# A transformer block on one core: seven products of quarters for eight in half of the second feed-forward

## The chip, the cores and the metric

The kernel runs on one core of a Trainium2 chip. The metric is the device time of one execution in microseconds. The kernel before takes 2150.8 us, the median of 3 runs (2146.12 to 2152.6).

## The reference

A block over 256 tokens of width 2048, in fp32: a gated feed-forward, a mixer (a state-space layer beside pooling), cross-attention to a memory of 256 rows, a second gated feed-forward, and a final norm. The change is in the second feed-forward alone, which is

```
def swiglu(x, w_gate, w_up, w_down):
    return (jax.nn.silu(x @ w_gate) * (x @ w_up)) @ w_down
h = h + 0.5 * swiglu(rmsnorm(h, g_ffn2[l]), w2_gate[l], w2_up[l], w2_down[l])
return rmsnorm(h, g_final)
```

with w_gate and w_up of 2048 x 5632 and w_down of 5632 x 2048.

## The kernel before, in words

The products are done in two rounded parts each. A weight tile of 512 input channels x 512 columns (1 MB) is loaded into one of three buffers `raw` by SyncE's queue. `wtile` splits it in two halves: for each, ScalarE rounds it to `whi` (L134) and VectorE subtracts what was rounded off, `wlo` (L135), both 128 x 1024 elements. `whi` and `wlo` have three buffers each, so three halves can be on the way. The activations are split in the same way, `xh` and `xl`, and stay in memory. `tok_block` then multiplies a channel block of 128 with both token tiles (lt = 0 and 1): xh x whi, xh x wlo, xl x whi, six matmuls of 512 columns in PSUM (L148 to L150). A half is two channel blocks, 12 matmuls; a unit of 512 channels is 24.

The feed-forward goes over 11 chunks f of 512 inner columns. A chunk's gate is four units over the 2048 channels (`tok_unit`), its up four more. ScalarE takes a tanh of the gate's sum (L302), VectorE makes the gated activation `s` from it (L304, L309), TensorE transposes `s` (L284, eight matmuls of 128 columns), and the two engines split the result into `x` tiles (L180, L181). After each two or three chunks (PASSES) come the down products: for each of four column groups one unit per chunk, whose sum VectorE adds to `h` (L256). The transposes are held back until the next unit has begun (`late`, `held`).

The order of the instructions on each engine is set when the kernel is built: a scheduler runs a model of the program and places each engine's instructions in the order in which they come up there. On the chip each engine then takes its own list strictly in that order.

Of the kernel before, what the change touches and what calls it, by code (L numbers as in the profile page):

```python
# [14 lines left out]
P = 128  # L15
# [7 lines left out]
FC = NQ  # L23
PASSES = ((0, 3), (3, 6), (6, 9), (9, 11))
# [29 lines left out]
def block_kernel(ctx: ExitStack, tc: tile.TileContext, xT, memT, wgu1, wd1, w_in, w_glu, w_pool, w_out,  # L54
# [10 lines left out]
    psA = ctx.enter_context(tc.tile_pool(name="psA", bufs=6, space=bass.MemoryType.PSUM))  # L65
    psB = ctx.enter_context(tc.tile_pool(name="psB", bufs=2, space=bass.MemoryType.PSUM))
# [60 lines left out]
    def wtile(load):  # L127

        raw = wraw.tile([P, 4, 512], F32, name="raw")
        load(raw)  # L130
        blocks = []
# [34 lines left out]
    def total(acc, out=None):  # L166
        b = ev.tile([P, L], F32, name="evb")
        S.activation(out=b, in_=acc[:, L:], func=AF.Copy)
        t = ev.tile([P, L], F32, name="evt", bufs=3) if out is None else out
        V.tensor_tensor(out=t, in0=acc[:, :L], in1=b, op=ALU.add)  # L170
        return t
# [85 lines left out]

    def ffn(fe, wgu, wd, xs, aside=None, begin=None, before=None, after=None):
# [21 lines left out]
        def transposed(ss, acts, t):  # L280
            pt = psB.tile([P, 2, L], F32, name="psb")
            for j in range(2):
                for lt in range(2):
                    T.transpose(pt[:, j, lt * P:(lt + 1) * P], ss[lt][:, (2 * t + j) * P:(2 * t + j + 1) * P], ident)  # L284
            for j in range(2):
                acts.append(split(ap_, pt[:, j]))

        for a, b in PASSES:
            acts = []
            for f in range(a, b):  # L290
# [4 lines left out]
                if f == 0:  # L295
                    norm_of_h()
                    V.tensor_scalar(out=hcol, in0=rcol, scalar1=0.5, scalar2=None, op0=ALU.mult)
                    V.tensor_scalar(out=qcol, in0=rcol, scalar1=0.25, scalar2=None, op0=ALU.mult)
                ss = []
                for lt in range(2):  # L300
                    th = fe.tile([P, 512], F32, name="th", bufs=2)
                    S.activation(out=th, in_=ag[lt], func=AF.Tanh, scale=hcol[:, lt:lt + 1])  # L302
                    s = fe.tile([P, 512], F32, name="s", bufs=4)
                    V.scalar_tensor_tensor(out=s, in0=th, scalar=1.0, in1=ag[lt], op0=ALU.add, op1=ALU.mult)  # L304
                    ss.append(s)
                if au is None:
                    au = tok_unit([cols4(wgu[4 * f:4 * f + 4, 1], i) for i in range(4)], xs, held())
                for lt in range(2):
                    V.scalar_tensor_tensor(out=ss[lt], in0=au[lt], scalar=rcol[:, lt:lt + 1], in1=ss[lt], op0=ALU.mult,  # L309
                                           op1=ALU.mult)  # L310
                late += [lambda ss=ss, t=t: transposed(ss, acts, t) for t in range(2)]
# [299 lines left out]
    kp = ExitStack()  # L611
    kT = kp.enter_context(tc.tile_pool(name="kp", bufs=1)).tile([P, KT, L], F32, name="kT")
    with ExitStack() as c2:
# [35 lines left out]
        def pool_in(n):  # L649
# [12 lines left out]
            q = ev.tile([P, L], F32, name="evs")  # L662
# [6 lines left out]
        def pool_out(g):  # L669
            wpb = load_w(w_pool[g], 512)  # L670
            for m in (2 * g, 2 * g + 1):
                acc = ntile(wpb[m % 2 * 2:m % 2 * 2 + 2], [pooled[2 * g], pooled[2 * g + 1]])
                b = ev.tile([P, L], F32, name="evb")
                S.activation(out=b, in_=acc[:, L:], func=AF.Copy, scale=vcol(P_SCALE + m))
                z = ev.tile([P, L], F32, name="evt", bufs=3)
# [135 lines left out]
        def gelu(j, slots):  # L811
# [6 lines left out]
            th = ev.tile([P, L], F32, name="evth")  # L818
# [41 lines left out]
        for n in range(8):  # L860
# [4 lines left out]
            th = ev.tile([P, L], F32, name="evth")  # L865
# [124 lines left out]
    with tc.tile_pool(name="fe2", bufs=2) as fe:  # L990
        o = fe.tile([P, KT, L], F32, name="o", bufs=1)

        def columns(n):
# [9 lines left out]
        ffn(fe, wgu2, wd2, xf, before=lambda i: layer_in(xf, ND - 1, G_FFN2, [xp] * KT) if i == 3 else None,  # L1003
            after=lambda n, i: columns(n - 1) if n > 0 and i == 1 else None)
# [87 lines left out]
```

## Time and profile before

| | |
|---|---|
| median of 3 runs | 2150.8 us |
| the profiled execution's own time | 2150.47 us |
| its span | 2148.7 us |
| TensorE busy | 2110.9 us (98%) |
| VectorE busy | 1305.9 us (61%) |
| ScalarE busy | 1012.1 us (47%) |
| DMA, mean | 199 GB/s |

The span runs from the first to the last instruction of the profiled execution. Busy time is the sum of the instructions' durations, with overlaps counted once. The second feed-forward lies between about 1406 us and 2132 us of the span. In the rows below PE is TensorE, PEld its weight loads, DVE VectorE, ACT ScalarE, SPq SyncE's queue of transfers; `acc` and `psb` are PSUM tiles.

### The profile page before, as it was taken

What the parts mean: (1) busy time and instruction counts of PE and PEld (TensorE: products, weight loads), DVE (VectorE), ACT (ScalarE), POOL (GpSimd) and SP (SyncE); (2) the same over time, 40 slices, a digit from 0 to 9 for tenths busy, and PEclk for the clock granted to TensorE, in tenths of its full rate; (3) what the DMA queues carried; (4) which work ended last, traced back from release to release, by engine and by line L of the source; (5) the groups of instructions that cost most, each with busy time, mean ns of one, the idle gap of its engine ahead of it and who ended that gap; (6) DMA issues with size and microseconds to landing.
All of it is one profiled execution on the core that took longest, in us unless ns stands there. A gap on an engine that the chain in (4) does not pass through costs nothing.

```text
span 2148.7 us, 26678 instructions
## 1 busy us (share of the span) xinstructions
PE 2110.9 (98%) x10356; PEld 1751.3 (82%) x10356; DVE 1305.9 (61%) x1793; ACT 1012.1 (47%) x1436; POOL 141.4 (7%) x255
## 2 busy tenths in 40 slices
PE   8999999999999999979999999999999999999997
PEld 7888888888888888867888888888888888888886
DVE  6567776766556667736867755555555555555554
ACT  7443444344444546524655644444434444444444
POOL 0000011111100011930000000000000000000000
PEclk9999999999999999989999999999999999999998
DMA  7666776777676666767554545566566656665662
GB/s 246 209 194 190 203 220 223 222 218 212 229 220 187 229 197 218 260 205 236 196 171 163 201 172 176 178 194 182 192 195 191 188 189 196 192 188 189 195 194 100
DMA packets 202320, 427.58 MB, mean 199 GB/s; under 512 B 17873, under 2 KB 31377, under 8 KB 193105
## 3 DMA queue, kind: packets, MB, share of 16 engines
q1 hardware_dynamic: 181280, 392.35, 58.9%
q0 software_dynamic: 6416, 18.85, 3.0%
q10 hardware_dynamic: 14496, 14.68, 2.2%
q8 instruction: 81, 1.33, 0.2%
q14 instruction: 47, 0.38, 0.0%
HBM read 408.05 MB, written 16.78 MB: 198 GB/s over the span
## 4 chain that ended last, share of the span: by engine, by line
PE 93%; POOL 3%; DMA 1%; DVE 1%; issue 1%; ACT 0%; SPq 0%; DVEq 0%; ACTq 0%
PE acc L150 25%; PE acc L148 25%; PE acc L149 25%; PE acc L116 7%; PE acc L117 4%; PE acc L968 1%; PE acc L969 1%; PE acc L967 1%; PE psb L284 1%; POOL big L728 1%; POOL rec L725 1%; POOL rec L726 1%; POOL rec L727 1%; PE psb L245 0%; DMA tab<-WTd 0%
## 5 line engine op out<-in xcount | busy, mean ns | idle before, releaser
L135 DVE TENSOR_TENSOR wlo<-raw,whi 128x1024 fp32r<-128x1024 f32 x576 | 705.9, 1226 | 600.0 <-ACT whi L134 598.0
L134 ACT ACTIVATE whi<-raw 128x1024 fp32r<-128x1024 f32 x576 | 610.9, 1061 | 785.0 <-PE acc L150 730.7
L149 PE MATMUL acc<-wlo,x 128*128 128x512 f32 x2368 | 925.0, 391 | 0.0
L150 PE MATMUL acc<-whi,x 128*128 128x512 f32 x2368 | 923.3, 391 | 0.0
L148 PE MATMUL acc<-whi,x 128*128 128x512 f32 x2368 | 843.8, 391 | 0.0
L150 PEld LDWEIGHTS acc<-whi,x 128*128 128x128 f32 x2368 | 444.8, 188 | 92.3 <-issue 1.2
L149 PEld LDWEIGHTS acc<-wlo,x 128*128 128x128 f32 x2368 | 445.0, 188 | 91.7 <-issue 0.4
L148 PEld LDWEIGHTS acc<-whi,x 128*128 128x128 f32 x2368 | 444.4, 188 | 91.5 <-issue 0.6
L116 PE MATMUL acc<-x,whi 128*128 128x512 f32 x848 | 301.4, 401 | 3.2 <-ACT whi L96 3.2
L97 DVE TENSOR_TENSOR wlo<-raw,whi 128x1024 fp32r<-128x1024 f32 (+1 forms) x144 | 172.0, 1199 | 125.9 <-ACT whi L96 110.0
L117 PE MATMUL acc<-x,wlo 128*128 128x256 f32 x848 | 235.8, 284 | 2.7 <-DVE wlo L97 2.6
L96 ACT ACTIVATE whi<-raw 128x1024 fp32r<-128x1024 f32 (+1 forms) x144 | 146.8, 1023 | 155.4 <-PE acc L116 78.1
L116 PEld LDWEIGHTS acc<-x,whi 128*128 128x128 f32 x848 | 159.0, 189 | 42.3 <-ACT whi L96 5.2
L117 PEld LDWEIGHTS acc<-x,wlo 128*128 128x128 f32 x848 | 159.5, 190 | 8.2 <-DVE wlo L97 5.3
L180 ACT ACTIVATE x<-psb 128x256 fp32r<-128x256 f32 x104 | 36.8, 376 | 46.3 <-PE psb L284 34.1
L181 DVE TENSOR_TENSOR x<-psb,x 128x256 fp32r<-128x256 f32 x104 | 41.5, 418 | 22.9 <-ACT x L180 22.8
L968 PE MATMUL acc<-wlo,x 128*128 128x512 f32 x128 | 50.1, 391 | 0.4 <-DVE wlo L97 0.4
L256 DVE SCALAR_TENSOR_TENSOR h<-acc,qcol,h 128x512 f32<-128x512 f32 x64 | 45.1, 743 | 6.7 <-PE acc L150 6.7
L969 PE MATMUL acc<-whi,x 128*128 128x512 f32 x128 | 48.8, 391 | 0.0
L967 PE MATMUL acc<-whi,x 128*128 128x512 f32 x128 | 47.9, 390 | 0.0
L302 ACT ACTIVATE th<-acc,hcol 128x512 f32<-128x512 f32 x44 | 30.0, 689 | 22.0 <-PE acc L150 22.0
L304 DVE SCALAR_TENSOR_TENSOR s<-th,acc 128x512 f32<-128x512 f32 x44 | 29.7, 685 | 8.4 <-ACT th L302 8.2
(218 smaller groups left out, 1079.4 us busy)
## 6 DMA issues: line engine op xcount, KB each, us to landing
raw<-in_wgu SPq DMA_DIRECT2D x175, 1024.0 KB, 5.9
raw<-in_wd SPq DMA_DIRECT2D x88, 1024.0 KB, 5.3
raw<-in_w_in SPq DMA_DIRECT2D x16, 1024.0 KB, 4.9
raw<-in_w_k SPq DMA_DIRECT2D x16, 1024.0 KB, 5.1
raw<-in_w_out SPq DMA_DIRECT2D x32, 512.0 KB, 4.9
raw<-in_w_q SPq DMA_DIRECT2D x16, 1024.0 KB, 4.8
raw<-in_w_v SPq DMA_DIRECT2D x16, 1024.0 KB, 4.9
raw<-in_w_o SPq DMA_DIRECT2D x16, 1024.0 KB, 5.1
```

The costliest lines, as they stand in the source:

```text
L96: S.activation(out=hi[:, :n], in_=r, func=AF.Copy)
L97: V.tensor_tensor(out=lo[:, :n], in0=r, in1=hi[:, :n].bitcast(F32), op=ALU.subtract)
L116: T.matmul(acc, w[0], x, start=first, stop=False)
L117: T.matmul(acc[:, :L], w[1], x[:, :L], start=False, stop=last)
L134: S.activation(out=hi, in_=raw[:, :, c:c + 256], func=AF.Copy)
L135: V.tensor_tensor(out=lo, in0=raw[:, :, c:c + 256], in1=hi.bitcast(F32), op=ALU.subtract)
L148: T.matmul(acc, xh, w[0], start=first, stop=False)
L149: T.matmul(acc, xh, w[1], start=False, stop=False)
L150: T.matmul(acc, xl, w[0], start=False, stop=last)
L967: T.matmul(accs[mt], mh, wh, start=k == 0, stop=False)
L968: T.matmul(accs[mt], mh, wl, start=False, stop=False)
L969: T.matmul(accs[mt], ml, wh, start=False, stop=k == KT - 1)
```

## The change

For the chunks f = 2 to 10 the first half of the channels (1024 of 2048) is computed with seven products for eight. The 256 tokens are two tiles, the 1024 channels two quarters of 512, and gate and up are the two column groups; that is a product of 2 x 2 by 2 x 2 blocks. Four of the seven products take differences of weight quarters, which VectorE makes in halves (`less`, L1050), and four take sums or differences of token tiles, which `token_sums` makes once (SH and SL). Each product (`product`) splits its weights into `whi` and `wlo` with `parts` as before, and is four channel blocks of three matmuls (L1057 to L1059). The products' results are added on VectorE, in SBUF (L1117, L1122 to L1124, L1139, L1143). The other half of the channels is done as before, in units (`eight`).

I name the pieces of a chunk in the order of the code: P1 (r11), D1, P2 (r12 - r11), D2, P3 (r22 - r12 + r11), D3, P4, D4, then E1 (gate), P5 (r21), E2 (up), P6 (r22), P7, E3 (gate), E4 (up). D1 to D4 are four down units of the two chunks before, which `seven` takes from the generator `down` one at a time (`step`); a and b are the two halves of each. The passes are now of two chunks, chunks 0 and 1 are computed without products, and the last pass has one chunk. PSUM is divided anew: four tiles `acc`, two `dacc` for the down sums, two `psb`.

```
+PASSES2 = ((0, 2), (2, 4), (4, 6), (6, 8), (8, 10), (10, 11))
...
+    banks.close()
+    psA = ctx.enter_context(tc.tile_pool(name="psC", bufs=4, space=bass.MemoryType.PSUM))
+    psB = ctx.enter_context(tc.tile_pool(name="psD", bufs=2, space=bass.MemoryType.PSUM))
...
+    def less(out, a, b):
+        for c in (0, 256):
+            V.tensor_tensor(out=out[:, :, c:c + 256], in0=a[:, :, c:c + 256], in1=b[:, :, c:c + 256], op=ALU.subtract)
+
+    def product(acc, w, x, first, last):
+
+        acc = acc.rearrange("p (f c) -> p f c", f=4)
+        for j, (wh, wl) in enumerate(parts(w)):
+            xh, xl = x(j)
+            T.matmul(acc, xh, wh, start=first and j == 0, stop=False)
+            T.matmul(acc, xh, wl, start=False, stop=False)
+            T.matmul(acc, xl, wh, start=False, stop=last and j == 3)
...
+            x = wraw.tile([P, 8, L], F32, name="raw")
+            for k in range(8):
+                V.tensor_tensor(out=x[:, k], in0=xf[k][:, :L].bitcast(F32), in1=xf[k][:, L:].bitcast(F32), op=ALU.add)
...
+            s = wraw.tile([P, 4, 4, P], F32, name="raw")
...
+            s1, s5, u2, u3 = (sw.tile([P, 512], F32, name=n) for n in ("s1", "s5", "u2", "u3"))
+            t = sw.tile([P, 4, 512], F32, name="t")
+            r11 = load(wraw, "raw", cols4(g, 0))
+            p = tmp()
+            product(p, r11, quarter(0, 0), True, True)
+            S.activation(out=s1, in_=p, func=AF.Copy)
+            step()
+            r12 = load(sw, "r12", cols4(u, 0))
+            less(t, r12, r11)
+            p = tmp()
+            product(p, t, tsum(0), True, True)
+            S.activation(out=s5, in_=p, func=AF.Copy)
+            step()
+            r22 = load(sw, "r22", cols4(u, 1))
+            less(t, r22, t)
+            p = tmp()
+            product(p, t, tsum(1), True, True)
+            V.tensor_tensor(out=u2, in0=p, in1=s1, op=ALU.add)
+            step()
+            less(r12, r22, r12)
+            p = tmp()
+            product(p, r12, tsum(2), True, True)
+            V.tensor_tensor(out=u3, in0=p, in1=u2, op=ALU.add)
+            V.tensor_tensor(out=u2, in0=u2, in1=s5, op=ALU.add)
+            V.tensor_tensor(out=s5, in0=u3, in1=s5, op=ALU.add)
+            step()
+            gate, up = ([psA.tile([P, 512], F32, name="acc") for _ in range(2)] for _ in range(2))
...
+            eight(gate, g, 2)
+            r21 = load(sw, "r21", cols4(g, 1))
+            product(gate[0], r21, quarter(4, 0), False, False)
+            eight(up, u, 2)
+            product(up[0], r22, tsum(3), False, False)
+            less(t, r21, t)
+            product(gate[1], t, quarter(4, 1), False, False)
+            eight(gate, g, 3)
+            gs_ = [sw.tile([P, 512], F32, name=f"gate{lt}") for lt in range(2)]
+            for lt, x in enumerate((s1, u3)):
+                V.tensor_tensor(out=gs_[lt], in0=gate[lt], in1=x, op=ALU.add)
+            ss = gated(fe, gs_)
+            eight(up, u, 3)
+            for lt, x in enumerate((u2, s5)):
+                V.tensor_tensor(out=gs_[lt], in0=up[lt], in1=x, op=ALU.add)
+            upped(ss, gs_)
+            finish_chunk(ss, acts)
...
-        ffn(fe, wgu2, wd2, xf, before=lambda i: layer_in(xf, ND - 1, G_FFN2, [xp] * KT) if i == 3 else None,
-            after=lambda n, i: columns(n - 1) if n > 0 and i == 1 else None)
+        for n, _ in enumerate(down(*PASSES2[-1], acts, done=squares)):
+            if n > 0:
+                columns(n - 1)
```

On VectorE, in the kernel before, this is the end of a chunk's up units and the beginning of the next chunk (s is the gated activation, x its transposed tiles):

```order
L135 TENSOR_TENSOR wlo_13844<-raw_13837,whi_13843 128x1024
L135 TENSOR_TENSOR wlo_13878<-raw_13875,whi_13877 128x1024
L135 TENSOR_TENSOR wlo_13882<-raw_13875,whi_13881 128x1024
L309 SCALAR_TENSOR_TENSOR s_13727<-acc_13733,rcol_92,s_13727 128x512
L309 SCALAR_TENSOR_TENSOR s_13731<-acc_13734,rcol_92,s_13731 128x512
L135 TENSOR_TENSOR wlo_13934<-raw_13931,whi_13933 128x1024
L135 TENSOR_TENSOR wlo_13938<-raw_13931,whi_13937 128x1024
L181 TENSOR_TENSOR x_13890<-psb_13885,x_13890 128x256
```

On VectorE, now, at the end of chunk 2: E3 (13279, 13283), E4 (13325, 13329), the half differences of chunk 3's t and r12 between them, and P1 of chunk 3 (13369, 13373):

```order
L140 TENSOR_TENSOR wlo_13279<-raw_13276,whi_13278 128x1024
L1050 TENSOR_TENSOR t_13364<-r12_13447,raw_13365 128x4x256 x2
L140 TENSOR_TENSOR wlo_13283<-raw_13276,whi_13282 128x1024
L1050 TENSOR_TENSOR r12_13447<-r22_13509,r12_13447 128x4x256
L140 TENSOR_TENSOR wlo_13325<-raw_13322,whi_13324 128x1024
L1050 TENSOR_TENSOR r12_13447<-r22_13509,r12_13447 128x4x256
L140 TENSOR_TENSOR wlo_13329<-raw_13322,whi_13328 128x1024
L1139 TENSOR_TENSOR gate0_13310<-acc_13140,s1_12867 128x512
L1139 TENSOR_TENSOR gate1_13311<-acc_13141,u3_12870 128x512
L140 TENSOR_TENSOR wlo_13369<-raw_13365,whi_13368 128x1024
L140 TENSOR_TENSOR wlo_13373<-raw_13365,whi_13372 128x1024
L275 SCALAR_TENSOR_TENSOR s_13316<-th_13314,gate0_13310 128x512
```

Where four splits stood side by side, four half differences now stand between them, and the additions of the products' sums follow. The list goes on with s, D1a (13416), two additions (L1143) and D1b (13420); then VectorE has, up to D2a (13476):

```order
L281 SCALAR_TENSOR_TENSOR s_13316<-gate0_13310,rcol_92,s_13316 128x512
L140 TENSOR_TENSOR wlo_13453<-t_13364,whi_13452 128x1024
L281 SCALAR_TENSOR_TENSOR s_13320<-gate1_13311,rcol_92,s_13320 128x512
L140 TENSOR_TENSOR wlo_13457<-t_13364,whi_13456 128x1024
L1050 TENSOR_TENSOR t_13364<-r22_13509,t_13364 128x4x256 x2
L140 TENSOR_TENSOR wlo_13476<-raw_13473,whi_13475 128x1024
L186 TENSOR_TENSOR x_13394<-psb_13389,x_13394 128x256
```

Both halves of P2 (13453, 13457) and the whole next difference stand ahead of D2a. On TensorE, at the same place, D2a (13475, into dacc) stands ahead of P2 (13452, into psb); these are its last two matmuls and P2's first three:

```order
L154 MATMUL dacc_13412<-wlo_13476,x_12904 128x512
L155 MATMUL dacc_13412<-whi_13475,x_12904 128x512
L1057 MATMUL psb_13451<-whi_13452,SH_12214 128x512
L1058 MATMUL psb_13451<-wlo_13453,SH_12214 128x512
L1059 MATMUL psb_13451<-whi_13452,SL_12215 128x512
```

So the two engines have the two pieces in opposite order. A little later on TensorE, at the end of P3 (13518) and the beginning of D3a (13539):

```order
L1059 MATMUL psb_13513<-whi_13518,SL_12215 128x512
L153 MATMUL dacc_13535<-whi_13539,x_12576 128x512
L153 MATMUL dacc_13536<-whi_13539,x_12576 128x512
L1057 MATMUL psb_13573<-whi_13574,SH_12214 128x512
L154 MATMUL dacc_13535<-wlo_13540,x_12576 128x512
L155 MATMUL dacc_13535<-whi_13539,x_12576 128x512
```

The first matmul of P4 (13574) stands in the middle of D3a, ahead of the first that reads D3a's wlo.

## Rows read from the trace of the kernel before

**Rows 1.** The page: busy time of each engine with its share of the span, and the share of the chain that ended last by engine.

```profile
PE 2110.9 (98%) x10356; PEld 1751.3 (82%) x10356; DVE 1305.9 (61%) x1793; ACT 1012.1 (47%) x1436; POOL 141.4 (7%) x255
...
PE 93%; POOL 3%; DMA 1%; DVE 1%; issue 1%; ACT 0%; SPq 0%; DVEq 0%; ACTq 0%
```

**Rows 2.** Two windows of 66 us in the second feed-forward: the stretch, its length, then each engine's busy time (instructions), the granted clock, the share of the DMA engines and GB/s.

```profile
1451.00:1517.00 66.00, 66.00 (x298) 54.66 (x297) 35.88 (x38) 30.36 (x36) 0.00 (x0) 1.00 0.65 191
1737.00:1803.00 66.00, 66.00 (x297) 54.66 (x296) 35.90 (x37) 26.66 (x28) 0.00 (x0) 1.00 0.60 187
```

**Rows 3.** The chain in order of time, second feed-forward: start, length, what.

```profile
1450.66 0.66 PE psb L284 x6
1457.02 0.45 PE acc L148 x2
1459.74 0.45 PE acc L148 x2
...
1495.11 0.65 PE psb L284 x6
```

**Rows 4.** The waits between 1450 and 2090 us: who waited for whom, in total, times, the longest.

```profile
ACT whi L134 <- PE acc L150: 326.2, 212, 1.7
DVE wlo L135 <- ACT whi L134: 284.3, 230, 1.5
```

**Rows 5.** The timeline around 1747 us: start, length, engine, line, operation, and in brackets the idle time before it and what ended it.

```profile
1746.90 0.39 PE L150 MATMUL acc<-whi,x 128*128 128x512 f32 x1
...
1747.13 0.62 PE L148 MATMUL acc<-whi,x 128*128 128x512 f32 x2
...
1747.39 1.06 ACT L134 ACTIVATE whi<-raw 128x1024 fp32r<-128x1024 f32 x1 [1.67 <-PE acc L150]
...
1748.48 1.23 DVE L135 TENSOR_TENSOR wlo<-raw,whi 128x1024 fp32r<-128x1024 f32 x1 [1.50 <-ACT whi L134]
...
1749.62 1.40 DVE L256 SCALAR_TENSOR_TENSOR h<-acc,qcol,h 128x512 f32<-128x512 f32 x2
```

**Rows 6.** Groups by line and shape from 1480 us to the end: count, total busy us, mean ns of one, idle time before.

```profile
L135 DVE TENSOR_TENSOR wlo<-raw,whi 128x1024 fp32r<-128x1024 f32 x234 | 286.6, 1225 | 284.9 <-ACT whi L134 284.5
L134 ACT ACTIVATE whi<-raw 128x1024 fp32r<-128x1024 f32 x233 | 247.0, 1061 | 336.6 <-PE acc L150 324.0 <-issue 12.4
...
L256 DVE SCALAR_TENSOR_TENSOR h<-acc,qcol,h 128x512 f32<-128x512 f32 x32 | 22.5, 744 | 6.7 <-PE acc L150 6.7
L181 DVE TENSOR_TENSOR x<-psb,x 128x256 fp32r<-128x256 f32 x40 | 15.9, 418 | 12.0 <-ACT x L180 12.0
...
L304 DVE SCALAR_TENSOR_TENSOR s<-th,acc 128x512 f32<-128x512 f32 x18 | 12.3, 687 | 4.0 <-ACT th L302 4.0
...
L1009 DVE TENSOR_TENSOR o<-o,Ra 128x1024 f32<-128x1024 f32 x4 | 4.6, 1218 | 1.8 <-ACT Ra L214 1.8
```

**Rows 7.** Timeline of VectorE, two pairs that start back to back (the length is that of the pair).

```profile
1423.98 1.28 DVE L304 SCALAR_TENSOR_TENSOR s<-th,acc 128x512 f32<-128x512 f32 x2 [0.84 <-ACT th L302]
...
1453.81 0.75 DVE L181 TENSOR_TENSOR x<-psb,x 128x256 fp32r<-128x256 f32 x2
```

**Rows 8.** TensorE waiting elsewhere in the kernel: three rows of the timeline around 1010 us (a matmul of 512 columns, a split, and the matmul that reads it), the window around them, the kernel's longest wait, and the window around that.

```profile
1009.22 0.39 PE L116 MATMUL acc<-x,whi 128*128 128x512 f32 x1
...
1010.02 1.22 DVE L97 TENSOR_TENSOR wlo<-raw,whi 128x1024 fp32r<-128x1024 f32 x1
...
1011.29 0.39 PE L117 MATMUL acc<-x,wlo 128*128 128x256 f32 x1 [1.68 <-DVE wlo L97]
...
1008.00:1012.00 4.00, 2.32 (x11) 1.63 (x11) 2.38 (x4) 1.76 (x4) 0.00 (x0) 1.00 0.19 49
...
933.58 0.70 PE L798 MATMUL psb<-tab,big 128*32 128x128 f32 x8 [11.62 <-DMA big<-big]
...
920.00:940.00 20.00, 8.38 (x73) 6.74 (x72) 2.79 (x3) 1.56 (x3) 10.77 (x29) 0.66 0.43 128
```

**Rows 9.** DMA issues between 1744 and 1800 us: count, KB each, median us from issue to landing.

```profile
raw<-in_wd SPq DMA_DIRECT2D x7, 1024.0 KB, 5.3
raw<-in_wgu SPq DMA_DIRECT2D x4, 1024.0 KB, 5.9
```

More of the change, by code (lines that the diff above doesn't have):

```diff
@@ L130, in wtile, with parts @@
         load(raw)
+        return parts(raw)
+    def parts(raw):
         blocks = []
@@ L278, in held @@
             return run
[L280 to L286, printed above, removed]
         for a, b in PASSES:
@@ L295, in ffn @@
                 if f == 0:
[L296 to L305, printed above, removed]
+                    ffn_norm()
+                ss = gated(fe, ag)
                 if au is None:
                     au = tok_unit([cols4(wgu[4 * f:4 * f + 4, 1], i) for i in range(4)], xs, held())
[L308 to L311, printed above, removed]
+                upped(ss, au)
+                late += [lambda ss=ss, t=t: act_tiles(ss, acts, t) for t in range(2)]
             for n in range(ND):
@@ L611, in block_kernel @@
     kp = ExitStack()
+    ev2 = kp.enter_context(tc.tile_pool(name="ev2", bufs=2))
     kT = kp.enter_context(tc.tile_pool(name="kp", bufs=1)).tile([P, KT, L], F32, name="kT")
@@ L987, in block_kernel, with flush @@
     kp.close()
-    with tc.tile_pool(name="fe2", bufs=2) as fe:
-        o = fe.tile([P, KT, L], F32, name="o", bufs=1)
+    banks.close()
+    psA = ctx.enter_context(tc.tile_pool(name="psC", bufs=4, space=bass.MemoryType.PSUM))
+    psB = ctx.enter_context(tc.tile_pool(name="psD", bufs=2, space=bass.MemoryType.PSUM))
+    fe = ctx.enter_context(tc.tile_pool(name="fe2", bufs=2))
+    gate_up = lambda f, m: wgu2[4 * f:4 * f + 4, m]
+    late = []
+    def flush(n=2):
+        for _ in range(min(n, len(late))):
+            late.pop(0)()
@@ new lines, in finish_chunk, with plain, first @@
+    def finish_chunk(ss, acts):
+        late.extend([lambda t=t: act_tiles(ss, acts, t) for t in range(2)])
+    def plain(f, acts, before=None):
+        def first(i):
+            flush()
+            if before is not None:
+                before(i)
+        ag = tok_unit([cols4(gate_up(f, 0), i) for i in range(4)], xf, first)
+        if f == 0:
+            ffn_norm()
+        ss = gated(fe, ag)
+        upped(ss, tok_unit([cols4(gate_up(f, 1), i) for i in range(4)], xf))
+        finish_chunk(ss, acts)
@@ new lines, in down @@
+    def down(a, b, acts, accs_of=tok_accs, done=None):
+        for n in range(ND):
+            accs = accs_of()
+            for i, f in enumerate(range(a, b)):
+                blocks = wtile(cols4(wd2[f, 4 * n:4 * n + 4], 0))
+                flush()
+                for j, w in enumerate(blocks):
+                    tok_block(accs, w, acts[4 * i + j], i + j == 0, f == b - 1 and j == 3)
+                if f == b - 1:
+                    add_to_h(accs, n, qcol)
+                    if done is not None:
+                        done(n)
+                yield
@@ L993, in columns @@
+    with tc.tile_pool(name="last", bufs=1) as last:
+        o = last.tile([P, KT, L], F32, name="o")
         def columns(n):
```

84 lines of the change are left out of this document (75 added, 9 removed).

## The prediction

> **What bounds the kernel now.** I read the page's busy times and its chain first [rows 1]: TensorE is busy for 98% of the span and carries 93% of the chain, VectorE is at 61%, ScalarE at 47%. Then the windows over two pieces of the second feed-forward [rows 2]: TensorE is busy for every one of the 66 us, at a granted clock of 1.00, VectorE for 36 of them. So there it runs on matmuls alone. The chain in order of time [rows 3] gives their price: the same pair of matmuls comes back every 2.72 us (1457.02, 1459.74), and 12 matmuls of 512 columns lie between, so a matmul costs 0.227 us. A chunk's gate and up take 44.45 us (1450.66 to 1495.11), eight transposes in it 0.88 (six of them 0.66); its down blocks are another 96 x 0.227 = 21.8. Sum 66.2 us per chunk.
>
> The waits [rows 4] say what the other engines do meanwhile: ScalarE waits 326 us for TensorE to hand back a weight buffer, VectorE 284 us for ScalarE. That is the slack the change spends. One turn of that loop is in [rows 5]: the last matmul of a half starts at 1746.90, the next half's first at 1747.13; ScalarE starts the next `whi` at 1747.39, which is 0.26 after; it takes 1.06; VectorE starts `wlo` 0.03 later (1748.48) and needs 1.23. From a buffer handed back to a usable `wlo` are 2.6 us.
>
> **What it removes.** Per chunk f = 2 to 10 seven products of 12 matmuls stand for eight: 12 x 0.227 = 2.72 us less. Nine chunks: 24.5 us off TensorE's path.
>
> **What it adds on VectorE.** I name a chunk's pieces: P1 to P7 the products (2.72 us of TensorE each), E1 to E4 the plain units of the other channels (5.44 each), D1 to D4 the woven down blocks (5.44 each), a and b their halves. Before, a chunk had 24 halves to split, now 30, and 8 half differences at L1050, 8 additions of a product's sum, and no other engine takes any of it. The split lasts 1.225 us, the same shape without rounding 1.218 [rows 6]; but back to back they start closer: 1748.48 to 1749.62 is 1.14 [rows 5]. The trace has no L1050; its bounds are 0.59 from below (a shape half as long, the step of the pair at 1423.98 [rows 7]) and 1.23; same shape, engine and memory as `wlo`, so I take 1.14. The 128x512 operations step by 0.59 to 0.66 (pairs of 1.28 and 1.40 less one duration [rows 5 to 7]): 0.63. The transposed tiles step by 0.33 (0.75 less 0.42 [rows 6, 7]). A chunk: 38 x 1.14 + 16 x 0.63 + 4 x 0.33 = 54.7 us, against TensorE's 276 x 0.227 + 0.9 = 63.5. On the average VectorE fits. The question is where.
>
> **Where it doesn't fit (A).** Three weight buffers let VectorE be at most three halves ahead. Take T = 0 when TensorE has done P6. E3a's buffer comes free then, so its `wlo` starts at 0.26 + 1.06 + 0.03 = 1.35. From there the order gives VectorE, without a wait that would be later: E3, E4, P1, D1, P2 and D2a (11 splits), six half differences, and eight 128x512 operations. That is 17 x 1.14 + 8 x 0.63 = 24.4 us; with the last one's full duration and 0.05 to reach TensorE (VectorE ends at 1011.24, TensorE starts at 1011.29 [rows 8]) D2a's `wlo` is there at 25.9. TensorE meanwhile has P7, E3, E4, P1, D1 = 21.8, eight transposes 0.9, two matmuls of D2a 0.45: it stands at 23.1, because D2a is in its order before P2, whose weights have long been ready. Stall 2.8 us. In eight chunks, 3 to 10; before chunk 2 the plain units leave VectorE time, and I count 0.
>
> **The second place (B).** T = 0 when D2a resumes. TensorE: ten matmuls 2.27, P2, D2b and P3 8.16, two of D3a 0.45, one of P4: at 11.1 it wants D3a's `wlo`. VectorE: P3a's buffer, P2a's, is free at 3.63, so its `wlo` starts at 4.98; with P3b, two half differences, two additions to `h` (1.40) that makes D3a's start 4.98 + 4 x 1.14 + 1.3 = 10.9, its end 12.2. Stall 1.1. Even with VectorE quick, P4a's `whi`, which TensorE wants ahead of that, uses P3b's buffer: free at 10.43, ready 1.35 later, wanted at 10.88: 0.9. I take 1.2, in nine chunks. In the chunks where D2b takes P2a's buffer some 0.4 more: 0.2 a chunk on the mean.
>
> **Small things.** The token sums take two of three raw buffers, so one weight load is issued only when the last split of the load before ends, and lands 5.3 to 5.9 us later [rows 9]; with `whi` and `wlo` 8 us, while TensorE has two halves and two matmuls, 5.9, in hand: 2 us, once. The first transposes of the feed-forward follow right on the output projection, so they wait for `h`: 0.3 + 0.74: 1. The last pass has one chunk instead of two, so ScalarE's squares and copies crowd: 1. The loads of r12, r21 and r22 each wait for the last split that reads the old one; r22's is the latest, three us ahead of its use, and I cost it at nothing; if it lands late, VectorE stands still with all its splits behind it. The additions at L1139 wait for E3's last matmul, which has ended some two us before VectorE gets to them: nothing. POOL does nothing here. In the tail nothing is removed.
>
> **Sum.** Against the profiled execution's own time, 2150.5 us (span 2148.7; median of the runs shown 2150.8, no difference): 2150.5 - 24.5 + 8 x 2.8 + 9 x 1.2 + 9 x 0.2 + 2 + 1 + 1 = 2165. A chunk goes from 66.2 to 67.6: it saves 2.7 and waits 4.2. I forecast **2165 us, slower**.
>
> **Rivals.**
> *It simply saves.* VectorE has 54.7 of 63.5 us, and before it waited half its time; if its lead at E3 is larger than three buffers allow on my reading, or the half differences step near their lower bound (8 x 0.55 = 4.4 us less a chunk, more than both stalls), the time is 2150.5 - 24.5 + 4 = 2130. Against it: the buffers' handing back is what VectorE waits for in [rows 4].
> *It cancels.* The operations of A step by 5 to 10% less than I take (1.2 to 2.4 of 24.4 us), B stays, since the buffer alone makes 0.9 of it: 2165 - 8 x 1.2 = 2155 down to 2165 - 8 x 2.4 = 2146, some 2150. For it: the bounds of L1050 lie wide. Against: it is `wlo`'s shape.
> *Slower still: VectorE's operations don't overlap.* Place: the same two; with 1.23 a step instead of 1.14 the 17 + 6 operations of A and B take 2.1 us more, each of it a stall: 2165 + 8 x 2.1 = 2182. It decides from 1.17 a step on (then 2171). For it: several of these operations wait for the one just before them (the difference reads what was just written). Against: all 1.14 in the trace are of pairs that wait for ScalarE too.
> [...]
> [...]
> That the seven products are not fewer matmuls is excluded: the order has 108 fewer of 512 columns.
>
> **How the numbers follow.** Forecast 0.50 (its own range 2157 to 2176), saves 0.20, cancels 0.14, no overlap 0.11, clock 0.05. A measurement of this kernel can tell about 0.3%, 6.5 us, from no change: 2144 to 2157. Faster 0.21 (saves, and the low end of cancels), same 0.15, slower 0.64. The range cuts half of the saving case and the worst of the slow ones: 2136 to 2184.
>
> **What would show it.** In the profile after: TensorE waiting for `wlo` at the matmuls of `dacc`, some 2.8 us once in each chunk with the transposes just ahead, and some 1.2 us at `dacc` or at the product of r12; 67 to 68 us from one chunk's transposes to the next; VectorE without idle time over some 24 us before each long wait; L1050 at 1.2 us. Wrong if TensorE's waits sum to under 15 us, if they are for DMAs, or if the chunk is 64 us.

## The result, and the profile after

The changed kernel takes 2176.1 us in the median of 4 runs (2173.0 to 2180.7), against 2148.6 for the kernel before (2146.1 to 2152.6). The ratio is 1.0128, 95% interval 1.0102 to 1.0155: slower by about 27 us. The forecast was 2165, slower, with 2136 to 2184 as its range. The direction came out as forecast. The size is 11 us short, at the very end of the likeliest case's own range (2157 to 2176).

The profiled execution has a span of 2172.8 us. Its page, as in [rows 1], first the busy time of each engine, then the shares of the chain that ended last:

```profile
PE 2104.4 (97%) x10248; PEld 1733.9 (80%) x10248; DVE 1504.0 (69%) x2021; ACT 1080.7 (50%) x1510; POOL 141.5 (7%) x255
...
PE 86%; DVE 5%; POOL 3%; issue 2%; ACT 2%; DMA 1%; SPq 0%; DVEq 0%; ACTq 0%
```

TensorE runs 108 matmuls fewer (10356 to 10248), as the change says. VectorE has 198 us more to do and now carries 5% of the chain, where it had 1%. On the average it is still far from full (69%). The two windows of [rows 2], with the same columns, show that the average hides where it is full:

```profile
1451.00:1517.00 66.00, 65.31 (x292) 53.56 (x290) 48.14 (x49) 31.79 (x37) 0.00 (x0) 1.00 0.61 180
1737.00:1803.00 66.00, 62.33 (x273) 49.96 (x272) 54.38 (x57) 33.46 (x38) 0.00 (x0) 1.00 0.61 181
```

In the first window little is lost (before, TensorE was never idle there). In the second, deep in the feed-forward, TensorE is idle for 3.67 us and starts 273 matmuls instead of 297 in the same 66 us.

The waits from 1440 to 2100 us, as in [rows 4] (who waited for whom: us in total, times, the longest):

```profile
ACT whi L139 <- PE dacc L155: 121.2, 67, 3.8
DVE wlo L140 <- ACT whi L139: 117.7, 114, 3.9
...
PE dacc L154 <- DVE wlo L140: 17.6, 13, 2.0
...
PE psb L1057 <- ACT whi L139: 5.9, 9, 0.7
```

Read the second row against its counterpart in [rows 4]. VectorE waited 284 us for ScalarE's `whi`; now it is 118. That slack was spent. The third and fourth rows are new: TensorE waits for `wlo`, and for the `whi` of P4, which it did nowhere in the feed-forward before.

The timeline around the first of these places, stall A of chunk 3 (start, length, engine, line, operation; in brackets the idle time before it and who ended it). L140 is the split's subtraction, L153 to L155 the matmuls of a down block, L287 the transposes, L1050 a half difference:

```profile
1564.59 1.22 DVE L140 TENSOR_TENSOR wlo<-t,whi 128x1024 fp32r<-128x1024 f32 x1
...
1565.25 1.03 PE L287 MATMUL psb<-ident,s 128*128 128x128 f32 x8
1565.45 1.06 ACT L139 ACTIVATE whi<-raw 128x1024 fp32r<-128x1024 f32 x1 [1.66 <-PE dacc L155]
...
1565.73 2.35 DVE L1050 TENSOR_TENSOR t<-r,t 128x1024 f32<-128x1024 f32 x2
...
1566.56 0.73 PE L153 MATMUL dacc<-whi,x 128*128 128x512 f32 x2 [0.28 <-ACT whi L139]
1568.00 1.21 DVE L140 TENSOR_TENSOR wlo<-raw,whi 128x1024 fp32r<-128x1024 f32 x1
...
1569.27 0.77 PE L154 MATMUL dacc<-wlo,x 128*128 128x512 f32 x1 [1.97 <-DVE wlo L140]
...
1570.27 0.63 PE L154 MATMUL dacc<-wlo,x 128*128 128x512 f32 x1
1570.69 0.63 PE L155 MATMUL dacc<-whi,x 128*128 128x512 f32 x1
```

This is the picture that the prediction drew for D2a: eight transposes, two matmuls on D2a's `whi` (1566.56), then nothing until its `wlo`, which VectorE begins only at 1568.00 because the two half differences for P3 stand ahead of it. The bracket of 1.97 understates the loss, since it counts from the pair's end in the trace (1567.29), which is 0.28 behind two steps of 0.2267. Counted from starts, the pair at 1566.56 should be followed 0.45 us later, and is followed 2.71 us later: 2.26 lost. The pair itself is 0.47 late. Together 2.73 us.

VectorE over the 24.8 us before that restart, same columns as the other windows:

```profile
1544.50:1569.27 24.77, 22.52 (x104) 18.20 (x102) 24.53 (x27) 12.82 (x15) 0.00 (x0) 1.00 0.55 187
```

It is busy for 24.53 of 24.77 us, in 27 operations. But for 0.17 us ahead of the first that starts there it hardly waits; it works through its queue. Below, two of these operations, neither of which waits for anything:

```profile
1548.16 1.22 DVE L140 TENSOR_TENSOR wlo<-raw,whi 128x1024 fp32r<-128x1024 f32 x1
1549.30 1.22 DVE L1050 TENSOR_TENSOR r<-r,r 128x1024 f32<-128x1024 f32 x1
```

The duration is 1.22 us and the step from one start to the next 1.13 to 1.15.

VectorE's queue is not the whole of A. D2a takes the weight buffer that D1's second half has just handed back: ScalarE waits for that and writes the `whi` from 1565.45 to 1566.51. With VectorE free at that moment its `wlo` would be ready at about 1567.8 (0.03 to start, 1.22, 0.05 to reach TensorE). TensorE would want it at 1566.5, which is 0.45 behind the undelayed start of the pair (1566.09). So of the 2.73 us some 1.5 are, by this estimate, the two half differences' and some 1.3 the buffer's, which TensorE's order brings out by taking D2a straight behind D1. In chunk 2, where P2 stands between them and VectorE has less to do, there is no stall A.

Stall B, some 12 us behind A in the same chunk (L1057 is the first kind of matmul of a product, here P4's):

```profile
1581.61 0.62 PE L153 MATMUL dacc<-whi,x 128*128 128x512 f32 x2
...
1581.94 2.35 DVE L140 TENSOR_TENSOR wlo<-raw,whi 128x1024 fp32r<-128x1024 f32 x2
1582.92 0.50 PE L1057 MATMUL psb<-whi,SH 128*128 128x512 f32 x1 [0.69 <-ACT whi L139]
1583.26 0.46 PE L154 MATMUL dacc<-wlo,x 128*128 128x512 f32 x1
```

P4's first matmul comes 1.31 us behind the start of D3a's pair, of which 0.45 is the pair's own: 0.86 lost. It waits for `whi` by name, and in chunks 4, 6, 8 and 10 D3a's `wlo` then costs 0.94 more.

**Where the time went.** Taking every start of TensorE from 1395 to 2110 us against a step of 0.2267 us for 512 columns (0.105 for a transpose), the kernel before loses about 1 us and the changed one 46.8 us more (such a sum is good to a microsecond or so):

| term | forecast, us | read after, us |
|---|---|---|
| A | 8 x 2.8 = 22.4 | 8 x 2.73 = 21.8 |
| B | 9 x 1.2 = 10.8 | 9 x 0.86 + 4 x 0.94 = 11.5 |
| D2b, where it takes P2a's buffer | 1.8 | 4 x 0.32 = 1.3 |
| wait behind the token sums, once | 2 | 1.7 |
| first transposes wait for `h` | 1 | 0.45 + 0.48 = 0.9 |
| clock low behind A | 0 | 3 x some 1.6 = 4.7 |
| the four products on sums of tokens, slower step | 0 | 2.6 |
| many steps of 0.1 and less | 0 | 2.2 |
| tail, behind 2110 us | 1 | 2.3 |
| sum | 39.0 | 49.1 |

Less the 24.5 us saved that is 24.6 us, and the two spans differ by 24.1. From one chunk's transposes to the next are 68.0 to 70.3 us, 69.0 in the mean (1566.56 to 2049.41 in seven steps), against 66.2 before and the 67 to 68 that the prediction named as its sign.

### The profile page after: what moved, and what is told of

It reads as the page before. It is cut to its first block, busy times and chain, and to the rows that moved or that the text cites. A ratio compares the mean times of both kernels' runs of the same rounds, so it can differ in the third digit from the quotient of the medians.

```text
span 2172.8 us, 26801 instructions
## 1 busy us (share of the span) xinstructions
PE 2104.4 (97%) x10248; PEld 1733.9 (80%) x10248; DVE 1504.0 (69%) x2021; ACT 1080.7 (50%) x1510; POOL 141.5 (7%) x255
## 3 DMA queue, kind: packets, MB, share of 16 engines
q8 instruction: 80, 1.31, 0.2%
## 4 chain that ended last, share of the span: by engine, by line
PE 86%; DVE 5%; POOL 3%; issue 2%; ACT 2%; DMA 1%; SPq 0%; DVEq 0%; ACTq 0%
PE acc L153 18%; PE acc L155 18%; PE acc L154 18%; PE acc L118 7%; PE acc L119 4%; PE dacc L154 3%; PE dacc L155 3%; DVE wlo L140 2%; PE dacc L153 2%; PE acc L984 1%; PE acc L985 1%; PE acc L983 1%; PE psb L1057 1%; PE acc L1057 1%; PE acc L1059 1%
## 5 line engine op out<-in xcount | busy, mean ns | idle before, releaser
L140 DVE TENSOR_TENSOR wlo<-raw,whi 128x1024 fp32r<-128x1024 f32 x522 | 636.0, 1223 | 376.2 <-ACT whi L139 373.8
L154 PE MATMUL acc<-wlo,x 128*128 128x512 f32 x1760 | 688.4, 391 | 0.0
L155 PE MATMUL acc<-whi,x 128*128 128x512 f32 x1760 | 686.8, 391 | 0.0
L153 PE MATMUL acc<-whi,x 128*128 128x512 f32 x1760 | 628.2, 392 | 1.8 <-ACT whi L139 1.6
L153 PEld LDWEIGHTS acc<-whi,x 128*128 128x128 f32 x1760 | 330.3, 188 | 70.9 <-ACT whi L139 2.0
L155 PEld LDWEIGHTS acc<-whi,x 128*128 128x128 f32 x1760 | 330.9, 188 | 69.2 <-issue 1.2
L154 PEld LDWEIGHTS acc<-wlo,x 128*128 128x128 f32 x1760 | 331.1, 188 | 68.4 <-issue 0.4
L154 PE MATMUL dacc<-wlo,x 128*128 128x512 f32 x320 | 127.9, 402 | 18.0 <-DVE wlo L140 17.6
L155 PE MATMUL dacc<-whi,x 128*128 128x512 f32 x320 | 125.4, 396 | 0.0
L153 PE MATMUL dacc<-whi,x 128*128 128x512 f32 x320 | 114.8, 398 | 4.1 <-ACT x L185 2.2
L140 DVE TENSOR_TENSOR wlo<-r,whi 128x1024 fp32r<-128x1024 f32 x54 | 66.1, 1223 | 35.8 <-ACT whi L139 34.6
L154 PEld LDWEIGHTS dacc<-wlo,x 128*128 128x128 f32 x320 | 60.7, 191 | 37.0 <-DVE wlo L140 24.5
L140 DVE TENSOR_TENSOR wlo<-t,whi 128x1024 fp32r<-128x1024 f32 x54 | 65.7, 1222 | 19.8 <-ACT whi L139 19.5
L153 PEld LDWEIGHTS dacc<-whi,x 128*128 128x128 f32 x320 | 60.0, 190 | 19.7 <-ACT x L185 3.1
```

What stands on the lines that cost most here:

```text
L140: V.tensor_tensor(out=lo, in0=raw[:, :, c:c + 256], in1=hi.bitcast(F32), op=ALU.subtract)
L153: T.matmul(acc, xh, w[0], start=first, stop=False)
L154: T.matmul(acc, xh, w[1], start=False, stop=False)
L155: T.matmul(acc, xl, w[0], start=False, stop=last)
```

## The experiments

My theory after this result: the whole loss comes of VectorE's queue. The half differences stand in it in one place, each ahead of a split that TensorE wants sooner, and D2a and D3a pay. The rivals: the weaving of down blocks between products costs something by itself, the loads or buffers do, or TensorE's order of D2a before P2 is what makes the stall. For each run, the ratio is to the kernel before on the same chip.

### e1: all the weaving, eight products

The seven products are put back to eight, with the down blocks woven between them as in the changed kernel, and without token sums.

```diff
-            r11 = load(wraw, "raw", cols4(g, 0))
-            product(p, r11, quarter(0, 0), True, True)
...
+            for i in range(2):
+                eight(gate, g, i)
+                step()
+                eight(up, u, i)
+                step()
```

> Eight products as before, but woven with the down blocks, in the new passes and the new division of PSUM; no differences, no token sums. Theory (VectorE late at two places a chunk): the 24.5 us of the products come back, and no wait of TensorE at the down blocks is left. Against the kernel before only the start (0.9) and the end (some 2.5) of the feed-forward cost: 2152 us (2149 to 2156). Rival (the weaving, the passes and the PSUM tiles cost it): 2165 or more, with waits of TensorE at dacc as in the changed kernel.

Measured: 2150.3 us, ratio 1.0003 (0.9994 to 1.0013). The second window of [rows 2] in this kernel:

```profile
1737.00:1803.00 66.00, 66.00 (x297) 54.80 (x296) 36.18 (x36) 27.75 (x31) 0.00 (x0) 1.00 0.62 191
```

TensorE is full again, with the same 297 matmuls, and VectorE has the 36 us of before. Weaving costs nothing that shows. The loss belongs to the seven products.

### e2: the seven products without their differences

The half differences (L1050) are left out, so the products read the raw quarters. Everything else is the changed kernel.

```diff
-            less(t, r12, r11)
-            product(p, t, tsum(0), True, True)
+            product(p, r12, tsum(0), True, True)
...
-            less(t, r22, t)
...
-            less(r12, r22, r12)
...
-            less(t, r21, t)
```

> Leaves the weight differences out of the computation (L1050): the products read r12, r22, r12 and r21 as loaded. All seven products, their splits and their additions stay. Theory: 8 x 1.14 us less on VectorE in a chunk, so the wait of 2.7 at D2a and VectorE's part of the second wait go, and the lowered clock with them: 2176 - 21.8 - 5 - 4 = 2145 us (2140 to 2150). Rival (the additions of the products' sums, or the three weight buffers with products of half the length, are the cause): 2160 or more.

Measured: 2136.5 us, ratio 0.9937 (0.9918 to 0.9956). That is below what I expected, since I had counted P4's `whi` as late by 0.9 us in every chunk because of the buffer. The two rows of TensorE's matmuls in the waits of 1440 to 2100 us are all that is left:

```profile
PE acc L153 <- ACT whi L139: 1.3, 1, 1.3
PE dacc L153 <- DVE h L261: 0.8, 1, 0.8
```

Neither is A or B. But VectorE is not all that changed. The scheduler sets every engine's order anew for each kernel, and here TensorE has P2 ahead of D2a, and P4's first matmul behind D3a and two of D3b instead of in the middle of D3a. In chunk 3 (D3a's first two, ScalarE's `whi` for P4, P4's first matmul):

```profile
1576.20 0.62 PE L153 MATMUL dacc<-whi,x 128*128 128x512 f32 x2
...
1576.40 1.06 ACT L139 ACTIVATE whi<-r 128x1024 fp32r<-128x1024 f32 x1 [0.34 <-PE psb L1059]
...
1579.41 0.40 PE L1057 MATMUL psb<-whi,SH 128*128 128x512 f32 x1
```

P4's `whi` is ready at 1577.46. In the changed kernel's order TensorE would ask for it at 1576.66, so the buffer's 0.8 us would be there with VectorE on time as well; the new order asks 2.75 us later. So e2 shows that without the differences no large wait is left, and not that the differences alone made all of A and B. From the last matmul ahead of the feed-forward to its last matmul this kernel takes 716.7 us, the one before 732.2, so it loses 9 us of the 24.5 saved; from 1395 to 2085 us no three of its matmuls in a row start some 0.43 us apart, as they do where the changed kernel's clock is low, and the products on sums of tokens still cost 2.6 (below). The loads of r12, r21 and r22, which are all still there, cost nothing.

### e3 and e7: only TensorE's order

If D2a's place ahead of P2 is the fault, P2 can be put first. In e3 the first matmul of a woven down block (D2 to D4) is held behind the product that stands before it in the program; e7 holds the products in the program's order as well. Both leave out the `flush()` in `step` too; in the trace the transposes stand where they stood, behind D1.

```diff
-            T.matmul(acc, xh, w[0], start=first, stop=False)
+            i = T.matmul(acc, xh, w[0], start=first, stop=False)
+            if pin:
+                tc.keep_in_program_order(i)
```

> Nothing but TensorE's order: the down blocks D2 to D4 stay behind the product in front of them, so that P2 comes before D2a; VectorE's order at that place as it was. Theory: TensorE wants D2a's wlo 2.72 us later, when it is just there: the 8 waits of 2.7 go to about 0.1, with them the lowered clock (5 us), the second wait grows a little: 2176 - 21 - 5 + 2 = 2152 us (2148 to 2158). Rival (VectorE has too much to do in the chunk as a whole): the wait comes up at the next split, the time stays at 2170 to 2177.

> As the kernel with the down blocks held behind the products, and the products too held behind the down blocks, so that P4's first matmul no longer stands in the middle of D3a. Theory: the wait for P4's whi (0.86 in each chunk) goes where VectorE is not later than it; where VectorE is, D3a's wait for wlo stays: 0 to 5 us under the kernel with the down blocks alone held, 2147 to 2153 us. Rival (that wait is VectorE's alone): the same time within 1 us.

Measured: e3 2195.8 us, ratio 1.0211 (1.0190 to 1.0231); e7 2194.7 us, 1.0207 (1.0187 to 1.0226). Both theories missed. TensorE's largest wait in e3, and the place in chunk 3 (in e3 L188 is the tile `x` of the transposes on VectorE, L1056 a difference, L1063 a product's first kind of matmul):

```profile
PE psb L1063 <- DVE x L188: 34.3, 8, 4.3
```

```profile
1564.74 2.35 DVE L1056 TENSOR_TENSOR t<-r,t 128x1024 f32<-128x1024 f32 x2
...
1567.01 1.22 DVE L140 TENSOR_TENSOR wlo<-raw,whi 128x1024 fp32r<-128x1024 f32 x1
1568.15 0.42 DVE L188 TENSOR_TENSOR x<-psb,x 128x256 fp32r<-128x256 f32 x1
...
1569.01 0.76 DVE L188 TENSOR_TENSOR x<-psb,x 128x256 fp32r<-128x256 f32 x2 [0.45 <-ACT x L187]
1569.58 0.47 PE L1063 MATMUL psb<-whi,SH 128*128 128x512 f32 x1 [4.29 <-DVE x L188]
```

P2's weights are ready, as the prediction said, but its result needs a `psb` tile of PSUM. There are two, and both hold transposes until VectorE has read them (1568.15 and after), which stands behind the same two differences and D2a's `wlo`. So P2 waits longer than D2a did: 4.48 us lost by starts in each of these chunks, against 2.73. Behind the stall in chunk 3 matmuls start 0.42 us apart (1570.21 and 1570.63), and the granted clock of the profiled execution is 0.983 in the mean, against 0.993 in the changed kernel. P2 first is no cure as long as the transposes stand right ahead of it: both pieces that could stand there needed something that VectorE had in its queue behind the differences.

### e8: the same work in another order, on VectorE and on TensorE

All products and all differences stay. The two of r22 less t go behind D2a's split, those of r22 less r12 behind D3a's split, those of r21 less t behind E1's second. On TensorE, P3 and P4 stay behind the piece before them, and each down block's second half behind the product before it. `behind` adds a dependence for the order alone.

```diff
-            less(t, r22, t)
+            less(t, r22, t, los[0])
...
-            product(p, t, tsum(1), True, True)
+            product(p, t, tsum(1), True, True, True)
...
-            less(r12, r22, r12)
+            less(r12, r22, r12, los[0])
...
-            less(t, r21, t)
+            less(t, r21, t, after_e1)
```

> All seven products and all differences, correct, but VectorE's differences are spread: r22 - t behind D2a's first split, r22 - r12 behind D3a's, r21 - t behind E1's second; on TensorE P3 and P4 stay behind the unit in front of them and each down block's second half behind the product in front. Theory (not the amount of VectorE's work but its place makes the waits): VectorE then enters P1 with two differences less behind it, no wait at D2a or D3a is left, the clock stays up; the time is that of the kernel without differences, 2136.5, plus little: 2137 to 2144 us, faster than the kernel before. Rival (8 differences more than VectorE can carry): waits of the same sum come up elsewhere, 2160 or more.

Measured: 2137.3 us, ratio 0.9944 (0.9929 to 0.9959): faster than the kernel before by 12 us and than the changed one by 39. First the page's busy times, then all rows of TensorE's matmuls in the waits from 1440 to 2110 us, then the second window:

```profile
PE 2096.6 (98%) x10248; PEld 1730.9 (81%) x10248; DVE 1502.4 (70%) x2021; ACT 1080.7 (50%) x1510; POOL 142.4 (7%) x255
```

```profile
PE psb L1066 <- DVE x L195: 1.4, 8, 0.2
PE acc L162 <- ACT whi L147: 1.3, 1, 1.3
PE dacc L162 <- DVE h L270: 0.8, 1, 0.8
PE dacc L163 <- DVE wlo L148: 0.2, 1, 0.2
```

```profile
1737.00:1803.00 66.00, 65.83 (x292) 53.46 (x291) 56.98 (x59) 36.27 (x40) 0.00 (x0) 1.00 0.64 194
```

Engine by engine the instructions are as many as in the changed kernel (VectorE 2021). VectorE is even busier in this window (56.98 of 66 us, against 54.38), and TensorE is idle for 0.17 us instead of 3.67. So the cost lay in the order of the pieces and not in the amount of VectorE's work.

Which order, this run does not say. TensorE's is another too: seven of the eight transposes are issued within D1, and P2 (1568.10) stands ahead of D2a (1570.97), so that D2a's buffer is free in time and P2's `psb` tile nearly so:

```profile
1564.68 0.93 PE L296 MATMUL psb<-ident,s 128*128 128x128 f32 x7
...
1568.10 0.47 PE L1066 MATMUL psb<-whi,SH 128*128 128x512 f32 x1 [0.17 <-DVE x L195]
...
1570.97 0.63 PE L162 MATMUL dacc<-whi,x 128*128 128x512 f32 x2
```

No run moves the pair r22 less t alone, with TensorE's order as in the changed kernel. By the estimate at stall A that would take away about half of it.

### e9: only the last pair of differences moved

Of e8's edits only one: r21 less t behind E1's second split. In the changed kernel that pair stands where it delays D3a's `wlo`.

```diff
-            less(t, r21, t)
+            less(t, r21, t, after_e1)
```

> The changed kernel with only the last difference, r21 - t, put later: behind E1's second split in place of around D3a's. Theory: the wait of 2.7 at D2a stays in all eight chunks; VectorE's part of the wait at D3a (0.9 in every second chunk) goes, some 0.9 a chunk for whi stays: 2168 to 2174 us. Rival (that wait has nothing to do with VectorE): 2175 to 2178.

Measured: 2167.1 us, ratio 1.0077 (1.0061 to 1.0094). The theory's place is right and its time was 1 us too high at the near end. A is left as it was: 2.73 us in each of eight chunks. B is gone, and its `whi` part, which was to stay, with it. VectorE's part went because D3a's `wlo` is now written in time (in chunk 3 from 1577.01, ahead of D3a's first matmul at 1578.28). The `whi` part went because TensorE's order changed as in e2: P4's `whi` is ready at 1579.53, and its first matmul, now behind D3a, comes at 1581.46. TensorE's largest wait, and a window of 4 us from A's restart on (the granted clock is the third figure from the end, ahead of the DMA share):

```profile
PE dacc L163 <- DVE wlo L148: 15.2, 11, 2.0
```

```profile
1565.96:1569.96 4.00, 4.00 (x11) 3.17 (x12) 1.46 (x4) 1.14 (x4) 0.00 (x0) 0.62 0.00 0
```

In this profiled execution the clock was low behind all eight stalls A: 0.62 and 0.57 in the 4 us from the restarts at 1565.96 and 1702.89, and behind each of the eight the slow steps add up to 1.6 to 1.7 us. That took back a good part of what the end of B gave: 11.5 of B went away, 5 more low stretches of some 1.6 came in, and from the last matmul ahead of the feed-forward to its last matmul e9 takes 750.5 us against the changed kernel's 755.6.

### e10: P4's first matmul out of D3a

The other cause that I could think of for B was TensorE's order: P4's first matmul stands in the middle of D3a and waits for a `whi`, with D3a's matmuls queued behind it. Here it is held until D3b is done.

```diff
-            product(p, r12, tsum(2), True, True)
+            product(p, r12, tsum(2), True, True, True)
```

> The changed kernel with only P4's first matmul put behind D3b, so that TensorE no longer asks for P4's whi in the middle of D3a. If the wait of 0.86 there is the buffer's alone, it goes in nine chunks: 2166 to 2170 us. If VectorE is as late with D3a's wlo, as its times in the changed kernel's trace say (it ends 1.1 us after TensorE would want it), the wait only changes its name, from whi to wlo: 2174 to 2179 us.

Measured: 2178.7 us, ratio 1.0128 (1.0110 to 1.0145), as the second of the two expectations had it. The wait goes over to D3a's `wlo`, at a slightly higher price: 1.15 us in chunks 3, 5, 7 and 9 and 2.03 in 4, 6, 8 and 10, against 0.86 and 1.80. It changes its name in the list:

```profile
PE dacc L154 <- DVE wlo L140: 26.1, 18, 2.0
```

The 5.9 us of `PE psb L1057 <- ACT whi` are gone from the list and 8.5 have come to the row of `wlo`. So two things were late at one place, and the list named one: with the buffer's wait out of the way VectorE's `wlo` was still as late. Chunk 2 tells them apart. VectorE is hardly behind there, and e10 loses 0.34 us at D3a, while the changed kernel loses 0.85 at P4's `whi` as in every other chunk: that is the buffer's. So my theory was too narrow. VectorE's queue is one part of A and B, and the weight buffers, under the order that TensorE has, are the other.

### e4: TensorE kept at work ahead of A

To see what the clock does when TensorE waits less: the eight transposes ahead of A are issued three times, so that 16 more (1.7 us) stand where TensorE would have waited.

```diff
-        for j in range(2):
-            for lt in range(2):
-                T.transpose(...)
+        for _ in range(times_):
+            for j in range(2):
+                for lt in range(2):
+                    T.transpose(...)
```

> The changed kernel with each transpose of the gated activations issued three times into the same tile, 16 more a chunk, 1.8 us of work for TensorE just ahead of its wait at D2a. Theory of the clock: TensorE then waits 1.0 us instead of 2.7 and the granted clock stays at 1.00 in all eight chunks, where it fell in three of eight; the time is 0 to 5 us less, 2171 to 2176, because the repeated work lies inside the wait. Rival (the wait is not the clock's cause): the clock falls in some chunks as before. If the wait is not there, the 16 transposes cost 1.8 us in each of 11 chunks: 2194.

Measured: 2173.5 us, ratio 1.0107 (1.0089 to 1.0125). The stall falls to 1.03 us, and behind none of the eight do three matmuls in a row start some 0.43 us apart; the clock is 1.00 in the 4 us behind the first and the sixth. The first of them:

```profile
1569.99:1573.99 4.00, 4.00 (x17) 3.31 (x18) 1.71 (x5) 2.11 (x5) 0.00 (x0) 1.00 0.00 0
```

In the changed kernel the same windows, from A's restart on in chunks 3, 4 and 8, have:

```profile
1569.27:1573.27 4.00, 4.00 (x11) 3.16 (x12) 1.46 (x4) 1.04 (x3) 0.00 (x0) 0.57 0.00 0
1638.58:1642.58 4.00, 4.00 (x17) 3.30 (x18) 1.46 (x4) 1.44 (x4) 0.00 (x0) 1.00 0.00 0
...
1913.56:1917.56 4.00, 4.00 (x11) 3.14 (x12) 1.46 (x4) 1.04 (x3) 0.00 (x0) 0.57 0.00 0
```

The time alone doesn't settle the price of the clock. The additional transposes are issued in 11 chunks and are hidden only in the eight with a stall, so three times 1.7, about 5 us, is paid, as much as the low stretches cost (4.7), and the intervals of the two kernels overlap. What the rows show is that with TensorE at work for longer ahead of a shorter wait no low stretch came at all, while in chunks 3 and 8 of the changed kernel 11 matmuls started in the 4 us in place of 17. The third low stretch of the changed kernel is behind A of chunk 7 (0.69 in the 4 us from 1844.29).

## Why the prediction was right, and where it was short

**What it removes, and on what engine the cost falls.** Right. 108 matmuls went, no wait for the loads of r12, r21 and r22 came (VectorE waited once, 0.6 us, for r11's), and the large new waits are for VectorE's `wlo` and for P4's `whi`, as it named them. e1 shows it by taking the products away, e2 by taking the differences away, e8 by moving them.

**A.** Right in place and size, 2.73 us against 2.8 in eight chunks, and in what ended last: VectorE's queue. It did not see that D2a's buffer would have cost about 1.3 of it with VectorE on time, a floor that hid behind VectorE's lateness. It cost the forecast nothing, but it means that a VectorE on time would not have ended the stall. The step of 1.14 for the half differences, taken from `wlo`, is what they take; this also decides the rival that VectorE's operations don't overlap: one lasts 1216 to 1223 ns in the mean of its form, and the steps are 1.13 to 1.15 us, so that rival's 2182 didn't come. But the rival's own reason, that one operation waits for the one just before it, was not tested at A: as far as the names tell, none of the 17 there reads or overwrites what the operation just before it handled. Where one does, at L1124, there was no overlap. It overwrites the `s` that L1123 has just read, and starts 0.72 us behind it, which lasts 0.68, in nine chunks of nine; the independent pairs of the same shape at L1139 and L1143 step by 0.60:

```profile
1593.69 0.68 DVE L1123 TENSOR_TENSOR u<-u,s 128x512 f32<-128x512 f32 x1
1594.41 0.69 DVE L1124 TENSOR_TENSOR s<-u,s 128x512 f32<-128x512 f32 x1
```

One sentence of A was wrong in what it implies: "D2a is in its order before P2, whose weights have long been ready". P2's weights were ready, but its PSUM tile was not (e3, e7). The order was no free choice of TensorE's.

**B.** Right in sum (11.5 against 10.8), and in both parts, though not in how they fall on the chunks: 0.86 in five and 1.80 in four, against 1.2 in each. P4's `whi` costs 0.86 in all nine chunks, chunk 2 too, where VectorE is hardly late: the 0.9 that the prediction put down to the buffer alone. VectorE's lateness at D3a was 1.15 in four chunks (e10) against 1.1, and larger in four others. What "Even with VectorE quick" took for granted is TensorE's order: in e2 and e9 the scheduler has P4's first matmul later, and the wait is absent. So the floor of 0.9 under the rival *It cancels* was there in the changed kernel; that rival failed because the operations of A didn't step by less.

**The clock.** This is the largest part of the 11 us. The forecast's sum puts the clock at nothing and leaves it to a case of its own, with a chance of 0.05. It came beside the likeliest case instead of in its place, in three chunks of eight, at some 1.6 us each. The step that fell short is the sum: with 1.84 us without a fall and 11.6 with one [rows 8], and a stall A of 2.8 between them, a term for the clock should have stood in the forecast itself. Behind 2.7 us lost it fell in 3 of 8 stalls here and in 8 of 8 in e9, behind 1.03 us in none of 8 (e4).

**The rest.** A matmul of the four products on token sums steps by 0.233 us instead of 0.227: 2.6 us that the prediction didn't have. The tail was 2.3 instead of 1: TensorE waits 0.99 at 2121 us for a `dacc` tile that VectorE has yet to add to `h`, where I had only the crowding of ScalarE's squares and copies. Some 2.2 us lie in small steps around the transposes and waits.

**It simply saves.** Not for this kernel. But e8 comes to 2137, not far from that rival's 2130: the slack for the differences is there, as the average of 54.7 in 63.5 us said. It isn't at the place where the change put them, with TensorE's pieces in the order that they had.

**What stays open.** How much of e8's 39 us is the place of the differences and how much TensorE's order: no run changes one without the other. Why the clock fell behind some stalls of the changed kernel and not behind others of the same length (chunks 3 and 4 above lose 2.73 us each). And what makes the products on token sums step by 0.233. None of these has a run of its own.

## What to carry to other kernels

An engine with time to spare on the average can still be late at every turn, as VectorE was here (69% busy over the span, 24.53 of 24.77 us ahead of stall A), where it takes its list in order (there P2's second `wlo`, the pair of differences, D2a's `wlo` and the first tile `x` start at 1564.59, 1565.73, 1568.00 and 1569.14, as they stand in the list) and the added work stands in one piece ahead of what the bound engine wants next. Ask for each added operation which later one it delays and by how much the buffers let that one run ahead, and spread the additions before giving the change up. Before an order is called wrong, see what else the piece to be put first needs (here a PSUM tile); and when a wait names one engine, ask what else would have been late at the same place, since the list names only what ended last. Where a scheduler sets the order, an edit for one engine can move the pieces of another: compare the orders of two kernels before a difference in time is put down to the edit.

## What the runs showed of the hardware that I had not expected

The granted clock fell behind a loss as short as 2.1 us. Behind stall A of chunk 3, 2.7 us, eight or so matmuls start 0.427 us apart (1570.27 and 1570.69 in the timeline of stall A) and then the step is some 0.23 again (1573.51 and 1573.74); the granted clock is 0.50 from 1569.80 to 1572.00 and 1.00 from 1573.00 to 1574.00. That costs 8 x 0.2 = 1.6 us. It happened in 3 of 8 stalls of the changed kernel's profiled execution, in 8 of 8 of e9's with the same stall, and in none of 8 where e4 left 1.03 us. The 2.1 us are in e8's profiled execution, at the place of [rows 8]: the matmul ahead of the wait starts at 1009.84, 2.10 are lost up to 1012.16, and the clock falls behind it. The changed kernel lost 2.05 at that place and the kernel before 1.84, both without a fall.

```profile
1012.16 0.38 PE L119 MATMUL acc<-x,wlo 128*128 128x256 f32 x1 [1.94 <-DVE wlo L99]
...
1013.00:1017.00 4.00, 4.00 (x16) 3.40 (x15) 4.00 (x7) 1.68 (x3) 0.00 (x0) 0.57 0.57 197
```

Matmuls of the same shape did not all step alike without a wait: 0.227 us and, on the token sums, 0.233, in the changed kernel's P3 of chunk 3 (1578.82 to 1581.61) at a granted clock of 1.00. In e8, the first matmul of P5 and of P6 and the first of the piece behind each:

```profile
1598.61 0.39 PE L1066 MATMUL acc<-whi,x 128*128 128x512 f32 x1
...
1601.33 0.61 PE L162 MATMUL acc<-whi,x 128*128 128x512 f32 x2
...
1606.78 0.40 PE L1066 MATMUL acc<-whi,SH 128*128 128x512 f32 x1
...
1609.58 0.40 PE L1066 MATMUL acc<-whi,x 128*128 128x512 f32 x1
```

P5 takes 2.72 us from its first start to the next piece's (1598.61 to 1601.33), P6 on the token sums `SH` and `SL` takes 2.80 (1606.78 to 1609.58) for the same 12 matmuls. In every kernel with these products, e2 without differences too, it adds up to some 2.6 us.
